# A layer's opening with four up blocks in turns over six PSUM banks, and one block's last rows inside the first seven-product block

## The chip, the cores and the metric

The kernel runs on one core of one Trainium2 chip. The metric is device time in microseconds, the median of several runs; a lower time is better. Of the engines, TensorE (PE, with PEld for its weight loads) multiplies, VectorE (DVE) and ScalarE (ACT) do the element-wise work, GpSimd (POOL) does small work and issues accumulating transfers, and SyncE (SP) issues the plain transfers in order.

## What is computed

One layer of a diffusion backbone on 256 latent tokens and 256 context tokens, width 2048, all in float32. The part that the change touches is the first half-step FFN with its modulation:

```python
mod_l = (silu_c @ w_mod[l] + b_mod[l]).reshape(B, N_MOD, D_MODEL)
mod_c = (silu_cc @ w_mod[l] + b_mod[l]).reshape(1, N_MOD, D_MODEL)
xl = half_step_ffn(xl, mod_l, 0, g_norm[l, 0], w_ffn1_up[l], w_ffn1_down[l])
xc = half_step_ffn(xc, mod_c, 0, g_norm[l, 0], w_ffn1_up[l], w_ffn1_down[l])

def half_step_ffn(x, mod, i, g, w_up, w_down):
    h = rms_norm(x, g) * (1 + mod[:, i + 1, None, :]) + mod[:, i, None, :]
    a, b = jnp.split(h @ w_up, 2, axis=-1)
    return x + 0.5 * mod[:, i + 2, None, :] * ((jax.nn.silu(a) * b) @ w_down)
```

Behind it come the token mixing (attention and mLSTM heads), a second FFN and a final RMSNorm, which the change leaves alone.

## The kernel before

**Products in three parts.** Every float32 operand is split into a rounded part hi and a rest lo (`split`: ACT makes hi, line 118, VectorE lo = raw - hi, line 119). A product of two split operands is three matmuls (`mm3`, lines 140 to 142): hi by hi, hi by lo, lo by hi. `split` draws from rings: three raw tiles of 1 MB, four hi and four lo tiles.

**The opening.** Context and latent tokens stand side by side as 512 columns. The 2048 rows of the width are 16 chunks of 128; `BLOCKS` takes them as (0,1), (1,2), (2,4), (4,6), ... (14,16). A block named by its first chunk k0 does this:

- *Modulation.* Shift SH and scale SC of its chunks come from `w_m0`, 32 units of 1 MB in the order of use (`mod_unit`, line 538, four buffers `mraw`). A pair block needs four units: one multiplied and summed on VectorE (the pair of 2.29 us operations), one for the other shift chunk and two for the scales, summed on PE with the conditions as stationary operand (`mod_sums`), copied by ACT to a row (line 558), transposed on PE and reduced on VectorE (`mod_turned`).
- *Hidden columns.* The normalised tokens `xs` are transposed on PE, and `affine_split` (lines 392 and 396) makes hhi (ACT) and hlo (VectorE) of them.
- *Up products.* `products` loads the block's rows of `w_up1` for both halves (a and b) of three hidden blocks f = 0, 1, 2 (line 425) and adds to six PSUM banks, one for each half of each f. A block's products run while the next block's modulation is made: six steps of six matmuls (three-matmul groups, pair by pair), put between the modulation sums.

In the opening VectorE, TensorE and the loads are pinned to program order (class `Pinned`, so their lines read L78); ACT is not. Before block 0 come the loads of the four token tiles, their sums of squares and scalings (`x_tile`), and `spread`, which broadcasts both conditions over the partitions: a diagonal on VectorE, four matmuls for each sequence, then copies to cB.

**Behind the opening.** `hidd` takes silu(a) * b of each f (`tail`, lines 666 to 668). The fourth block of the first group, f = 3, is loaded whole (line 133), split and multiplied in 96 matmuls. Then come nine groups of four hidden blocks by a seven-product scheme (`quad`); the first is called quad 1 here. It has 14 steps, each with a split and 24 matmuls; the operands a11, a12, a21, a22 are quarters of hhi and hlo, and n1, s2, s3, s4 are sums of them, made once by `token_forms` (lines 699 to 734) in 28 VectorE operations and some ACT copies: n1 ahead of quad 1, the others in its steps 1 to 6. n1 is used from step 4, s4 from step 6, s2 from step 8 and s3 from step 10. Its weights come in two `chain` tiles (`first_chain`, line 674), whose memory the opening's pool holds until its last operation, later added to by accumulating transfers from GpSimd (line 652). From here on a scheduler orders the instructions by readiness and program order.

## Time and profile before

| | us |
|---|---|
| median of 3 runs (lowest to highest) | 2656.78 (2656.41 to 2657.49) |
| profiled execution | 2654.22 |
| its span in the profile | 2652.5 |
| TensorE busy in the span | 2603.8 (98%) |
| VectorE busy | 2132.9 (80%) |
| ScalarE busy | 1349.5 (51%) |

The profile is of one execution. Busy time is the union of an engine's instructions; the profile models the ends of matmuls, which are pipelined. The views used are the page with its busy times, the table of windows (busy time, granted clock and DMA in chosen stretches), the groups of instructions with the idle time before them, the timeline and the waits of the transfer queue.

### The profile page before, as it was taken

To read this page: it belongs to the slowest core of one execution; us is meant where nothing else is said; L and a number is where in the kernel's file an instruction comes from. 1 tells how busy PE (TensorE), PEld (TensorE's weight loads), DVE (VectorE), ACT (ScalarE), POOL (GpSimd) and SP (SyncE) were. 2 spreads that over 40 slices of the span, in tenths; PEclk is the share of its full clock that TensorE was granted. 3 is DMA by queue.
4 is the path that set the end of the run, shared out by engine and by line. 5 is a ranking of instruction groups with operands and counts; after the bars stand their busy time and mean duration, and the time that the engine had idled before them with its cause. 6 is when DMAs were issued, how large, how long until landed. Compare 5 with 4: busy or idle time off the path is not lost. (4 is left out here: it accounts for less than half of the span.)

```text
span 2652.5 us, 33763 instructions
## 1 busy us (share of the span) xinstructions
PE 2603.8 (98%) x12718; PEld 2153.9 (81%) x12718; DVE 2132.9 (80%) x2918; ACT 1349.5 (51%) x1682; POOL 208.3 (8%) x259
## 2 busy tenths in 40 slices
PE   8999999999999999999999999999999999999998
PEld 4688887888888878888889888877898888888887
DVE  5697888878888788888886979797698777777877
ACT  4354444554444555444455336355476655555554
POOL 0000001000001100010110000111000000000001
PEclk9999999999999999999999999999999999999999
DMA  9979999999999988889986867574479998989975
GB/s 360 340 214 270 264 278 262 263 276 281 261 283 263 274 233 239 223 208 229 231 243 224 308 232 242 199 270 167 167 262 291 288 291 291 288 275 283 276 231 175
DMA packets 135028, 679.98 MB, mean 256 GB/s; under 512 B 14152, under 2 KB 23624, under 8 KB 73552
## 3 DMA queue, kind: packets, MB, share of 16 engines
q1 hardware_dynamic: 107216, 500.07, 50.8%
q0 software_dynamic: 27360, 177.22, 34.2%
q8 instruction: 100, 1.64, 0.2%
q10 hardware_dynamic: 288, 0.52, 0.1%
q14 instruction: 64, 0.52, 0.1%
HBM read 659.87 MB, written 17.89 MB: 256 GB/s over the span
## 5 line engine op out<-in xcount | busy, mean ns | idle before, releaser
L118 ACT ACTIVATE hi<-raw 128x1024 fp32r<-128x1024 f32 (+3 forms) x542 | 560.8, 1039 | 639.1 <-PE mm L142 481.8
L119 DVE TENSOR_TENSOR lo<-raw,hi 128x1024 fp32r<-128x1024 f32 (+1 forms) x524 | 631.1, 1211 | 272.2 <-ACT hi L118 254.9
L118 ACT ACTIVATE hi<-chain 128x1024 fp32r<-128x1024 f32 x320 | 337.9, 1059 | 257.6 <-PE mm L142 135.7
L119 DVE TENSOR_TENSOR lo<-chain,hi 128x1024 fp32r<-128x1024 f32 x320 | 387.5, 1221 | 95.8 <-ACT hi L118 93.1
L140 PE MATMUL mm<-hi,hhi 128*128 128x512 f32 (+3 forms) x1024 | 390.7, 384 | 7.3 <-DVE c L755 6.8
L141 PE MATMUL mm<-lo,hhi 128*128 128x512 f32 (+3 forms) x1024 | 387.6, 379 | 0.2
L142 PE MATMUL mm<-hi,hlo 128*128 128x512 f32 (+3 forms) x1024 | 387.0, 378 | 0.0
L211 DVE SCALAR_TENSOR_TENSOR junk<-sraw,cBh 128x1024 fp8e5<-128x1024 f32 x192 | 234.4, 1221 | 24.8 <-DMA sraw<-in_w_mt 22.5
L140 PEld LDWEIGHTS mm<-hi,hhi 128*128 128x128 f32 x1024 | 192.3, 188 | 40.0 <-ACT hi L118 6.4
L142 PEld LDWEIGHTS mm<-hi,hlo 128*128 128x128 f32 x1024 | 192.5, 188 | 33.6
L141 PEld LDWEIGHTS mm<-lo,hhi 128*128 128x128 f32 x1024 | 192.7, 188 | 32.0 <-DVE lo L119 1.3
L142 PE MATMUL mm<-hi,hid2l 128*128 128x512 f32 x352 | 137.4, 390 | 0.0
L140 PE MATMUL mm<-hi,hid2h 128*128 128x512 f32 x352 | 137.2, 390 | 0.0
L141 PE MATMUL mm<-lo,hid2h 128*128 128x512 f32 x352 | 137.1, 389 | 0.0
L140 PE MATMUL mm<-hi,h2hi 128*128 128x512 f32 x320 | 125.0, 391 | 1.5 <-DVE sab L1813 1.5
L141 PE MATMUL mm<-lo,h2hi 128*128 128x512 f32 x320 | 124.6, 389 | 0.0
L142 PE MATMUL mm<-hi,h2lo 128*128 128x512 f32 x320 | 124.6, 389 | 0.0
L652 POOL DMA_DIRECT2D chain<-in_w_up1b x60 | 53.1, 886 | 739.4 <-DVE lo L119 654.4
L142 PE MATMUL mm<-hhi,lo 128*128 128x512 f32 (+1 forms) x288 | 100.4, 349 | 4.5 <-DVE lo L119 4.4
L140 PE MATMUL mm<-hhi,hi 128*128 128x512 f32 (+1 forms) x288 | 101.3, 352 | 0.0
L141 PE MATMUL mm<-hlo,hi 128*128 128x512 f32 (+1 forms) x288 | 99.4, 345 | 0.0
L211 DVE SCALAR_TENSOR_TENSOR sr<-sr,cBl 128x1024 f32<-128x1024 f32 x72 | 87.1, 1216 | 7.0 <-DMA sr<-in_w_mt 6.8
(479 smaller groups left out, 5483.8 us busy)
## 6 DMA issues: line engine op xcount, KB each, us to landing
raw<-in_w_dn SPq DMA_DIRECT2D x70, 1024.0 KB, 7.3
sraw<-in_w_mt SPq DMA_DIRECT2D x128, 512.0 KB, 7.5
chain<-in_w_up1b POOLq DMA_DIRECT2D x60, 1024.0 KB, 11.1
raw<-in_w_up2b SPq DMA_DIRECT2D x50, 1024.0 KB, 7.0
raw<-in_w_up1b SPq DMA_DIRECT2D x40, 1024.0 KB, 8.5
sr<-in_w_mt SPq DMA_DIRECT2D x69, 512.0 KB, 5.3
mraw<-in_w_m SPq DMA_DIRECT2D x32, 1024.0 KB, 7.5
chain<-in_w_dn POOLq DMA_DIRECT2D x30, 1024.0 KB, 8.8
```

The costliest lines, as they stand in the source:

```text
L118: nc.scalar.activation(hi, src, AF.Copy)
L119: vector[0].tensor_tensor(lo, src, hi.bitcast(F32), op=ALU.subtract)
L140: tensor[0].matmul(out_ap, sh, mh, start=first, stop=False, skip_group_check=skip)
L141: tensor[0].matmul(out_ap, sh, ml, start=False, stop=False, skip_group_check=skip)
L142: tensor[0].matmul(out_ap, sl, mh, start=False, stop=last, skip_group_check=skip)
L211: ins = nc.vector.scalar_tensor_tensor(junk() if junk else raw, raw, 1.0, cB[s], op0=ALU.mult, op1=ALU.mult, accum_out=mT[:, i, s, kt, h : ...
L652: accum = lambda dst, src: nc.gpsimd.dma_start(dst, src, accum_op=ALU.add)
```

## The change

Four hidden blocks share the opening's six banks in turns. `COLUMN_PLAN` gives the blocks of f that each block of rows multiplies: 0, 1, 2 for rows up to chunk 4, then 1, 2, 3 up to chunk 10, then 2, 3, 0. When f = 0 has its chunks 0 to 3, and later f = 1 its chunks 0 to 9, the two banks are copied by ACT and written out to HBM by GpSimd (`PUT_BY`, `put_by`), and the banks go to f = 3 and to f = 0's second part. What a block missed is multiplied beside later blocks (`LATER`: f = 3's chunks 0 to 3 from block 6 on, f = 0's chunks 4 to 9 from block 12 on). The chunks 10 to 15 of f = 1 are multiplied within quad 1, in its steps 1 to 4, in two further PSUM banks. `whole_sums` copies a block's banks to SBUF and adds the part that was put by with an accumulating transfer; the tails of f = 0 and 1 then run at steps 4 and 7 of quad 1. The separate f = 3 goes.

`columns` takes the place of `products`: the same loads in one transfer where the f follow one another, else one for each f, and another order of matmuls: hi by hhi for all pairs of a load, then hi by hlo, then lo by hhi. The start of the opening is written out in `opening`: the first two modulation units are loaded ahead of block 0's weights, the latent condition is spread in four parts between other work, the sums of squares are shared by ACT and VectorE, and the scaling of each token tile beyond its first 256 columns is put off (`rest`) into the blocks 0 and 2.

```diff
 BLOCKS = ((0, 1), (1, 2)) + tuple((k, k + 2) for k in range(2, 16, 2))
+def _column_plan():
+    out = []
+    for k0, k1 in BLOCKS:
+        fs = (0, 1, 2) if k1 <= 4 else (1, 2, 3) if k1 <= 10 else (2, 3, 0)
+        out.append([[(f, k0, k1) for f in fs]])
+    return out
+COLUMN_PLAN = _column_plan()
+PUT_BY = {(0, 4): 3, (1, 10): 0}
+LATER = {6: [(3, 0, 4)], 12: [(0, 4, 8), (0, 8, 10)]}
 FB = 4
...
         return t if n == 2048 else t[:, :n]
-    def split(raw, n=2048):
-        half = n // 2
+    def split(raw, n=2048, count=2):
+        half = n // count
         parts = []
-        for h in range(2):
+        for h in range(count):
             hi = wp.tile([P, 1024], F32R, tag="hi", name="hi", bufs=4)[:, :half]
...
     pre = [[bank(), bank()] for _ in range(NPRE)]
+    slot = dict(enumerate(pre))
+    put_by = {f: [dr.tile([P, CB], F32, name=f"by{f}{ab}") for ab in range(2)] for f in (0, 1)}
     with pool(name="st", bufs=1) as st:
         scratch.append(st)
+        begun = set()
+        def columns(groups, early=False):
+            def load(g):
+                n = sum(2 * (k1 - k0) * P for _, k0, k1 in g)
+                raw = raw_tile(n)
+                o = 0
+                if len(g) > 1 and [f for f, _, _ in g] == list(range(g[0][0], g[0][0] + len(g))):
+                    f, k0, k1 = g[0]
+                    src = I["w_up1"][f : f + len(g), :, :, k0 * P : k1 * P].rearrange("f a p c -> p (f a) c")
+                    pin(nc.sync.dma_start(raw.rearrange("p (u c) -> p u c", u=2 * len(g)), src))
+                    return raw, n
+                for f, k0, k1 in g:
+                    w = 2 * (k1 - k0) * P
+                    pin(nc.sync.dma_start(raw[:, o : o + w].rearrange("p (a c) -> p a c", a=2), I["w_up1"][f, :, :, k0 * P : k1 * P].rearrange("a p c -> p a c")))
+                    o += w
+                return raw, n
+            ahead = load(groups[0])
+            if early:
+                wt = split(*ahead)
+            yield
+            for i, g in enumerate(groups):
+                if len(g) == 1:
+                    wt = split(*ahead, 1)
+                elif not early:
+                    wt = split(*ahead)
+                if i + 1 < len(groups):
+                    ahead = load(groups[i + 1])
+                each = [(f, ab, k) for f, k0, k1 in g for ab in range(2) for k in range(k0, k1)]
+                for f, _, _ in g:
+                    if f not in slot:
+                        slot[f] = [tbank(), tbank()]
+                done = 0
+                for wl, tl in ((0, 0), (0, 1), (1, 0)):
+                    for o, (f, ab, k) in enumerate(each):
+                        first = (f, ab) not in begun
+                        begun.add((f, ab))
+                        last = wl and (k == KT - 1 or (f, k + 1) in PUT_BY)
+                        tensor[0].matmul(slot[f][ab], wt(slice(o * P, o * P + P))[wl], (hhi, hlo)[tl][:, k, :], start=first, stop=bool(last))
+                        done += 1
+                        if done % (3 if g[0][2] - g[0][1] == 1 else 6) == 0:
+                            yield
+                for f, k0, k1 in g:
+                    if (f, k1) in PUT_BY:
+                        for ab in range(2):
+                            t = st.tile([P, 2, 256], F32, tag="h", name="by", bufs=2).rearrange("p a c -> p (a c)") if ab else st.tile([P, CB], F32, name="by", bufs=1)
+                            nc.scalar.activation(t, slot[f][ab], AF.Copy)
+                            nc.gpsimd.dma_start(put_by[f][ab], t)
+                            begun.discard((f, ab))
+                        del slot[f]
+                        slot[PUT_BY[f, k1]] = [bank(), bank()]
         cP = st.tile([P, KT, 32], F32, name="cP")
...
             return m
-        def spread(s, m):
-            for q in range(4):
-                b = pre[q // 2][q % 2]
-                w = slice(q * CB, (q + 1) * CB)
-                tensor[0].matmul(b, ones[:32, :], m[:, w], start=True, stop=True)
-                if s:
-                    nc.scalar.activation(cB[:, s, w], b, AF.Copy)
-                else:
-                    vector[0].tensor_copy(cB[:, s, w], b)
-        def x_tile(s, t, shared=False):
+        def spread(s, m, q, b):
+            w = slice(q * CB, (q + 1) * CB)
+            tensor[0].matmul(b, ones[:32, :], m[:, w], start=True, stop=True)
+            return lambda copy: copy(cB[:, s, w], b)
+        def x_sums(s, t, n_act):
             x = xs0[s, t]
...
             for cb in range(NCB):
-                if not (shared and cb % 2):
+                if cb < n_act:
                     sumsq(ss4[:, cb : cb + 1], x[:, cb * CB : (cb + 1) * CB])
...
             r = rsqrt_squares(ss4)
-            for c in (slice(0, 256), slice(256, D)):
-                vector[0].tensor_scalar(x[:, c], x[:, c], r, None, op0=ALU.mult)
+            return lambda c: vector[0].tensor_scalar(x[:, c], x[:, c], r, None, op0=ALU.mult)
         first_tb = pre[-1][-1]
...
                 tc.keep_in_program_order(nc.sync.dma_start(x, xsrc[s][t * P : (t + 1) * P, :]))
-        tc.keep_in_program_order(nc.sync.dma_start(vecs, I["vecs"]))
+        pin(nc.sync.dma_start(vecs, I["vecs"]))
         diagonals = [diagonal(s) for s in (CTX, LAT)]
-        spread(CTX, diagonals[0])
-        x_tile(CTX, 0)
-        x_turned(0, CTX, 0)
-        spread(LAT, diagonals[1])
-        for s, t in ((CTX, 1), (LAT, 0), (LAT, 1)):
-            x_tile(s, t, s == LAT and t == 1)
-            x_turned(0, s, t)
         def x_scaled(k, tb):
...
         unit = iter(range(32))
+        loaded = []
         def mod_unit():
+            if loaded:
+                return loaded.pop(0)
             raw = st.tile([P, 2048], F32, tag="mraw", name="mraw", bufs=4)
...
             turns.clear()
-        turns = []
-        for k0, k1 in BLOCKS:
+        turns, back, rest = [], iter(()), []
+        loaded.extend([mod_unit() for _ in range(2)])
+        def opening(following):
+            banks4 = [pre[q // 2][q % 2] for q in range(4)]
+            wide = [spread(CTX, diagonals[0], q, banks4[q]) for q in range(4)]
+            late = lambda q: spread(LAT, diagonals[1], q, (pre[2][0], banks4[0])[q] if q < 2 else tbank())(lambda o, x: nc.scalar.activation(o, x, AF.Copy))
+            for n, (s, t) in enumerate(xs0):
+                scaled = x_sums(s, t, 2 if n else 3)
+                wide[n](vector[0].tensor_copy)
+                scaled(slice(0, 256))
+                rest.append(lambda scaled=scaled: scaled(slice(256, D)))
+                if n == 3:
+                    drain(mod_sums(0, 0, 1))
+                x_turned(0, s, t)
+                for q in {1: (0,), 2: (1,)}.get(n, ()):
+                    late(q)
+            mod_turned()
+            drain(mod_sums(1, 0, 1))
+            steps(following)
+            mod_turned()
+            for q in (2, 3):
+                late(q)
+        for (k0, k1), groups in zip(BLOCKS, COLUMN_PLAN):
             kk = slice(k0, k1)
-            following = products(I["w_up1"], pre, k0, k1, hhi, hlo, k0 == 0)
+            following = columns(groups, k0 == 0)
+            if k0 in LATER:
+                back = columns([[x] for x in LATER[k0]])
+                steps(back)
             if k1 - k0 == 2:
                 raw = mod_unit()
-            for i in range(2):
+            if not k0:
+                opening(following)
+            for i in range(2 if k0 else 0):
                 for _ in mod_sums(i, k0 if i else k1 - 1, k1, following if i else iter(())):
                     steps(prods, 3 - (k1 - k0))
-                if k0 == 0:
-                    mod_turned()
+                    steps(back)
+                    if k0 == 2 and rest:
+                        rest.pop(0)()
                 if not i and k1 - k0 == 2:
...
             mod_turned()
+            while k0 == 2 and rest:
+                rest.pop(0)()
             steps(prods)
...
                 x_scaled(k0, tb)
+                if not k0:
+                    rest.pop(0)()
+                    rest.pop(0)()
             else:
...
         drain(prods)
+        drain(back)
         vector[0], tensor[0] = nc.vector, nc.tensor
...
             return f1u.tile([P, CB], F32, tag="ca", name="ca", bufs=2)
-        def tail(f, pab):
-            sa = ca_tile()
-            nc.scalar.activation(sa, pab[0], AF.Silu)
-            nc.vector.tensor_tensor(sa, sa, pab[1], op=ALU.mult)
+        def tail(f, a, b, sa):
+            nc.scalar.activation(sa, a, AF.Silu)
+            nc.vector.tensor_tensor(sa, sa, b, op=ALU.mult)
             nc.sync.dma_start(hidd[0][:, :, f, :], sa.rearrange("p (t c) -> p t c", t=4))
+        def whole_sums(f):
+            out = [c12_tile() if f else f1u.tile([P, CB], F32, tag="cy", name="cy", bufs=2) for _ in range(2)]
+            for x, b, before in zip(out, slot[f], put_by[f]):
+                nc.scalar.activation(x, b, AF.Copy)
+                accum(x, before)
+            return out
         def part(n, ab, c):
...
             first_chain(1, c)
-        for f in range(NPRE):
-            tail(f, pre[f])
-        for f in range(NPRE, FB):
-            pab = []
-            for ab in range(2):
-                wt = load_split(I["w_up1"][f, ab])
-                b = bank()
-                for k in range(KT):
-                    mm3(b, *wt(slice(k * P, (k + 1) * P)), hhi[:, k, :], hlo[:, k, :], k == 0, k == KT - 1)
-                pab.append(b)
-            tail(f, pab)
+        def c12_tile():
+            return f1u.tile([P, CB], F32, tag="c12", name="c12", bufs=2)
+        for f in (2, 3):
+            tail(f, *slot[f], ca_tile())
+        first_of = {0: whole_sums(0)}
         n1, s2, s4 = form("n", "n1"), form("s", "s2"), form("t", "s4")
...
         mul = lambda o, x, y: nc.vector.tensor_tensor(o, x, y, op=ALU.mult)
-        def c12_tile():
-            return f1u.tile([P, CB], F32, tag="c12", name="c12", bufs=2)
         def quad(n, after=lambda step: None):
...
         def first_steps(step):
+            if step == 0:
+                steps(back)
+            if step in (1, 2, 3):
+                steps(back, 2)
+            if step == 4:
+                drain(back)
+                tail(0, *first_of[0], first_of[0][0])
+                first_of[1] = whole_sums(1)
+            if step == 7:
+                tail(1, *first_of[1], first_of[1][0])
             if step in (1, 2, 3, 4, 5, 6):
...
         raws, place0 = [], []
+        back = columns([[(1, 10, 14)], [(1, 14, 16)]])
         quad(1, first_steps)
...
```

## The prediction

> **What bounds the kernel now.** I read the page first, for the engine that fills the span.
>
> ```profile
> span 2652.5 us, 33763 instructions
> PE 2603.8 (98%) x12718; PEld 2153.9 (81%) x12718; DVE 2132.9 (80%) x2918; ACT 1349.5 (51%) x1682; POOL 208.3 (8%) x259
> ```
>
> TensorE is busy for 98% of the span. A change that keeps its matmuls can only win the time in which it stands still. So the next view is the table of windows, cut at the starts of the opening's blocks and at the first seven-product block ("quad 1"). Its columns: window, its length, then for PE, PEld, DVE, ACT, POOL the busy time with a count, then clock, DMA share and GB/s.
>
> ```profile
> 0.00:29.60 29.60, 20.48 (x119) 9.10 (x119) 16.48 (x32) 17.00 (x43) 4.01 (x21) 1.00 0.92 358
> 29.60:46.50 16.90, 15.35 (x136) 9.58 (x136) 9.01 (x19) 4.82 (x11) 0.00 (x0) 0.90 0.90 339
> 46.50:61.00 14.50, 12.44 (x106) 8.17 (x106) 10.28 (x22) 5.09 (x10) 0.00 (x0) 1.00 0.97 370
> 61.00:74.70 13.70, 13.45 (x112) 9.21 (x111) 9.70 (x17) 5.09 (x10) 0.00 (x0) 1.00 1.00 370
> 102.00:116.80 14.80, 13.45 (x112) 9.21 (x111) 9.70 (x17) 5.09 (x10) 0.00 (x0) 1.00 0.98 354
> 130.50:144.10 13.60, 12.40 (x58) 9.83 (x57) 11.25 (x14) 6.10 (x11) 0.00 (x0) 1.00 0.55 209
> 144.10:166.00 21.90, 21.90 (x98) 18.16 (x97) 21.90 (x20) 10.39 (x12) 1.04 (x1) 1.00 0.82 242
> 166.00:242.00 76.00, 76.00 (x340) 62.95 (x340) 61.62 (x68) 37.62 (x42) 7.08 (x8) 1.00 0.86 232
> ```
>
> Three things stand here. In the opening PE is idle, most of it early. At the same time the DMA share is 0.90 to 1.00, so a block of 13.7 us is nearly full on both sides. And from 144.1 us PE has no idle time at all: block f=3 (144.1 to 166.0) and quad 1 run without a gap, but beside f=3 VectorE is busy for 21.90 of 21.90 us. Which waits make up the opening's idle time is in the groups of PE instructions from 0 to 144 us; the last part of a row is the idle time before the group.
>
> ```profile
> L78 PE MATMUL mm<-hhi,hi 128*128 128x512 f32 x96 | 41.9, 436 | 1.1 <-ACT hhi L392 1.1
> L78 PE MATMUL mm<-hhi,lo 128*128 128x512 f32 x96 | 38.8, 404 | 2.0 <-DVE lo L78 2.0
> L78 PE MATMUL mm<-hlo,hi 128*128 128x512 f32 x96 | 38.3, 399 | 3.0 <-DVE hlo L78 3.0
> L78 PE MATMUL tr<-mraw,cP 128*32 128x256 f32 x224 | 15.0, 385 | 1.9 <-DMA mraw<-in_w_m 1.9
> L78 PE MATMUL mm<-raw,ones 32*128 32x512 f32 x16 | 14.4, 1076 | 2.5 <-DVE raw L78 2.5
> L78 PE MATMUL tr<-mraw,cP 128*32 128x128 f32 x352 | 13.6, 302 | 0.3 <-DVE h L78 0.3
> L78 PE MATMUL tr<-ident,row 128*128 128x128 f32 x25 | 4.5, 277 | 0.8 <-ACT row L558 0.8
> L78 PE MATMUL mm<-ident,xs 128*128 128x128 f32 x4 | 1.4, 456 | 1.9 <-DVE xs L78 1.9
> L465 PE MATMUL tr<-ident,cc 32*128 32x32 f32 x1 | 0.3, 279 | 2.8 <-ACT cc L194 2.8
> ```
>
> Idle in all: 1.1+2.0+3.0+1.9+2.5+0.3+0.8+1.9+2.8 = **16.3 us**. The last row and the wait for the diagonals (2.5) come before anything the change touches, so 11.0 can be won. Busy spans are modelled past the next start, so gaps are somewhat longer than shown:
>
> ```profile
> 144.08 0.39 PE L140 MATMUL mm<-hhi,hi 128*128 128x512 f32 x1
> 144.30 0.39 PE L141 MATMUL mm<-hlo,hi 128*128 128x512 f32 x1
> 135.37 0.49 PE L78 MATMUL mm<-hlo,hi 128*128 128x512 f32 x1 [0.83 <-DVE hlo L78]
> 136.24 0.50 PE L78 MATMUL mm<-hhi,lo 128*128 128x512 f32 x1 [0.37 <-DVE lo L78]
> ```
>
> Streaming matmuls start 0.22 to 0.23 us apart, while one with a gap behind it is charged 0.49: each gap hides up to 0.27 us more, some 4 us over about 15 gaps.
>
> **The change part by part.**
>
> *The matmul count is conserved.* Before: 288 products in the opening (three groups of 96) and 96 for f=3. After, by the plan: f=0, 2, 3 get all 16 rows in the opening and f=1 ten, 58 rows of 6 matmuls = 348, and quad 1 takes the 6 missing rows, 36. At 0.227 us the opening grows by 60 x 0.227 = 13.6 us, quad 1 by 8.2, and the 21.8 us of f=3 go: zero. Spreads, modulation sums and transposes keep their number too. The whole effect is idle time won and lost.
>
> *Product order (hi by hhi for all pairs, then hlo, then lo): gain.* The waits for hlo and lo are 3.0+2.0 us. In a pair block 12 matmuls now stand ahead of the first that needs hlo (2.7 us) and 24 ahead of the first that needs lo (5.4 us); the longest wait, 0.83 us, is covered. With 0.27 us for nine such gaps this is 5.0+2.4 = 7.4 us at most. I take 5.5, since the early ones partly turn into waits for transfers (below).
>
> *Front: gain.* The first product starts at 29.60, where the first window ends; only after that does PE run steadily. In the new order PE no longer takes all eight spreads (14.4 us) before the first modulation sum; two go behind it, under the chain row, SC, hhi. I put the first product near 23.5 us. But 4 wide scalings and the second block's work meet on VectorE in block 2:
>
> ```profile
> L78 DVE TENSOR_SCALAR xs<-xs,rstd 128x1792 f32<-128x1792 f32 x4 | 4.6, 1148 | 0.0
> L78 DVE SCALAR_TENSOR_TENSOR junkv<-mraw,cB 128x2048 fp8e5<-128x2048 f32 x14 | 32.0, 2288 | 0.2
> 46.45 1.09 PE L78 MATMUL tr<-ident,xs 128*128 128x128 f32 x8
> ```
>
> Two scalings (2.3 us) stand in line with block 2's pair of 2.29 us sums ahead of its transposes (46.45 now). So of a lead of some 6 us about 4.2 is left there; I take **4.2**, bounds 2 and 6.
>
> *Transfers: loss.* The change adds to the opening 10 rows of reads (1.31 MB) and four partial sums out (1.05 MB): 2.36 MB at 370 GB/s = 6.4 us of a DMA that is 0.90 to 1.00 busy. All loads stand in SP's one ordered queue, so an added load delays the mraw units behind it.
>
> ```profile
> 56.81 1.07 PE L78 MATMUL tr<-mraw,cP 128*32 128x256 f32 x16 [0.77 <-DMA mraw<-in_w_m]
> 112.65 1.07 PE L78 MATMUL tr<-mraw,cP 128*32 128x256 f32 x16 [1.12 <-DMA mraw<-in_w_m]
> 126.29 1.07 PE L78 MATMUL tr<-mraw,cP 128*32 128x256 f32 x16
> 137.60 0.60 ACT L666 ACTIVATE ca<-mm 128x512 f32<-128x512 f32 x1 [2.41 <-PE mm L78]
> ```
>
> The front's lead pulls PE ahead of transfers that hardly can come sooner, so waits of about 1 us come in blocks 4 and 6 (where a 0.52 MB load and the first partial sums join). From block 8 on the 24 and then 36 extra matmuls (5.5 and 8.2 us) give the DMA more time than its extras take, and the 1.12 us wait goes. Sum **-0.7**, bounds 0 and -6. The opening's balance: 5.5+4.2-0.7 = **9.0 us won**, bounds 4 and 12. The added ACT copies (8 of about 0.6 us, half of them behind the opening) lie in ACT's idle time, which is over half of each block; uncovered they would cost 5.
>
> *The hand-over to quad 1: loss.* Today f=3's 21.9 us hide three things: the chains' landing, the tails, and the token forms on VectorE. That cover goes.
>
> ```profile
> 135.52 0.80 SPq L674 DMA_DIRECT2D chain<-in_w_up1b  x2
> 149.49 1.07 ACT L118 ACTIVATE hi<-chain 128x1024 fp32r<-128x1024 f32 x1 [0.28 <-PE mm L141]
> SPq L674 <- DVE hlo L78: 11.5, 1, 11.5
> DMA to landing us min/median/max: 4.8/7.2/8.2
> L119 DVE TENSOR_TENSOR lo<-chain,hi 128x1024 fp32r<-128x1024 f32 x8 | 9.7, 1220 | 0.5 <-ACT hi L118 0.5
> L699 DVE TENSOR_TENSOR sraw<-sraw,hlo 128x1024 f32<-128x1024 f32 x8 | 9.7, 1218 | 0.0
> L667 DVE TENSOR_TENSOR ca<-ca,mm 128x512 f32<-128x512 f32 x4 | 2.7, 680 | 0.0
> 151.51 1.22 DVE L119 TENSOR_TENSOR lo<-chain,hi 128x1024 fp32r<-128x1024 f32 x1
> 152.65 1.22 DVE L700 SCALAR_TENSOR_TENSOR sraw<-sraw,hhi 128x1024 f32<-128x1024 f32 x1
> ```
>
> Let H be the end of the last hlo. The chain load is issued 0.2 us after H, because it waits for hlo, and lands 4.8 us later at best: H+5.0. PE ends the last products about 7 us after H (36 x 0.227 = 8.2, begun 1.2 earlier). The first half's hi takes 1.07 (ACT) and lo 1.22 (VectorE): H+7.3 if VectorE is free, so nearly no wait. But from H it has 1.8 us of the block's own lo, then the first form n1, 8 operations at a pitch of 1.14 (151.51 to 152.65) = 9.1 us, and two tails, 1.2 us. All of these stand ahead of the first chain's lo in the program. If all go first, lo ends at H+13.3 and PE waits 6.3 us; if none, 0.5. The two halves of n1 wait for ACT between, so some lo slips in; nearest to the order seen in the trace, where VectorE runs forms as fast as they come, I take **4.5**.
>
> *Quad 1: small loss.* The two late loads bring 1.2 and 0.7 us of VectorE splits, four accumulating transfers go on POOL's queue (8% busy), and the four sums borrow the buffers of cy and c12, on which ACT's in-order copies may wait for a store. VectorE's work up to the eighth step (forms 28 x 1.14 = 32, splits 9 x 2.3 = 20, tails, adds) ends near H+57, PE gets there near H+59 (8 x 24 x 0.227 + 8.2 = 52 from H+7): close, but in time. I take **0.7**, bounds 0 and 3.
>
> Sum: -9.0+4.5+0.7 = **-3.8 us**. The profiled execution took 2654.22, 1.7 more than its span and 2.56 below the median 2656.78; the difference is put on the median: **2653.0**.
>
> One rule is weighed against this. The clock was cut once in the opening:
>
> ```profile
> 29.60:36.00 6.40, 5.59 (x43) 3.79 (x44) 1.22 (x2) 1.22 (x4) 0.00 (x0) 0.73 0.96 376
> ```
>
> It was granted 0.73 over these 6.4 us, after the idle stretches of the front, a loss of 1.7 us; no such cut follows at 144 us. A wait of 4 us or more at the hand-over could bring another 1.7; I leave it out of the sum and put it into the slower case. The Trainium skill ("TensorE: Matmul & The Clock Gate", "What's actually happening") says that an idle window of about 3.4 us halves the clock; by that rule the sum would be -2.1 instead of -3.8.
>
> **The rivals.**
> 1. *A clean hand-over.* VectorE takes the chain's lo as soon as it lands: wait 1.5, quad 1 at 0.3. -9.0+1.8 = -7.2: **2649.6**. For it: before, chain lo (151.51) ran in the middle of the forms. Against: program order.
> 2. *The opening is bound by transfers.* PE's lead is taken back by the mraw units behind 6.4 us of added traffic; the opening wins 4, the hand-over takes 4.5, quad 1 0.7: +1.2, **2658.0**. For it: shares of 0.97 to 1.00. Against: from the last unit's sums (126.29) PE still has some 18 us of work until 144.08.
> 3. *Slower: VectorE bounds quad 1.* The forms stay ahead of the splits: 6.3 at the hand-over and 1.7 of clock. VectorE then enters steps 3 to 6 without a lead, where it has 14 form operations (16.0), four splits (9.2) and some five adds and tails (3.0), 28.2 us, against PE's 4 x 24 x 0.227 = 21.8: 6.4 more. With 7.5 won in the opening: +6.9, **2663.7**. It decides where these losses pass the opening's gain by 5.3. For it: 21.90 of 21.90 us. Against: only n1 is due by step 4, and each step's split stands ahead of that step's form.
>
> **How the numbers follow.** Forecast 0.45, clean hand-over 0.30, transfers 0.15, slower 0.10. 0.2% is 5.3 us, about what a measurement of this kernel can tell from no change. Faster by more: the clean case and a fifth of the forecast's (0.39); slower by more: the last (0.10); the rest 0.51. The range goes from a won 10.5 (12 less 1.5) to a loss of 3: 2646.3 to 2660.0.
>
> **What would show it.** In the profile after: 348 and 36 products; hardly a row "<-DVE hlo" or "<-DVE lo" on PE before the hand-over; block 2's transposes near 42 us; the opening's products ending near 149 (144.1+13.6-9); then a PE gap before the first X matmul, put down to lo of the chain, of 3 to 6 us. The forecast is wrong if PE waits for mraw for more than 4 us in the opening, if that gap is under 2 us, or if PE waits again and again for lo within quad 1.

## The result and the profile after

The changed kernel took **2675.36 us** (median of 4 runs, 2670.83 to 2677.55), the kernel before 2656.6 beside it; the ratio is **1.0068** with a 95% interval of 1.0056 to 1.008. It is slower by 18.8 us; the forecast of 2653.0 and its range to 2660.0 are missed. The profiled execution took 2674.02 us; a trace is of one execution, and those of one kernel differ by some microseconds.

The profile's page of the changed kernel: TensorE has the same 12718 matmuls, and the span is 19.8 us longer.

```profile
span 2672.3 us, 33819 instructions
PE 2613.6 (98%) x12718; PEld 2160.8 (81%) x12718; DVE 2136.0 (80%) x2929; ACT 1349.0 (50%) x1681; POOL 213.1 (8%) x267
```

The table of windows, cut again at the blocks' starts and behind the opening (columns as in the prediction):

```profile
0.00:28.80 28.80, 23.06 (x119) 9.99 (x119) 16.00 (x39) 13.76 (x32) 4.00 (x21) 1.00 0.93 368
46.00:63.50 17.50, 13.54 (x105) 9.08 (x106) 10.28 (x22) 6.15 (x11) 0.00 (x0) 0.90 0.96 369
108.50:132.60 24.10, 19.41 (x130) 13.78 (x129) 10.83 (x18) 6.81 (x13) 1.07 (x2) 0.86 0.88 332
132.60:149.90 17.30, 17.30 (x130) 12.66 (x129) 10.30 (x18) 5.09 (x10) 0.00 (x0) 1.00 0.12 49
162.00:193.00 31.00, 26.06 (x104) 20.02 (x103) 27.75 (x27) 16.77 (x20) 3.57 (x4) 0.94 0.99 281
193.00:250.00 57.00, 51.40 (x213) 41.70 (x214) 44.03 (x49) 25.73 (x30) 7.01 (x8) 0.94 0.91 225
```

Before, PE was busy without a gap and at full clock from 144.1 to 242 us. Now it lacks 4.9 us in the 31 after the opening and 5.6 in the next 57, at a clock of 0.94. In the opening the stretch in which block 12's modulation is made (108.5 to 132.6) has a hole and a clock of 0.86, and right behind it the transfers stand nearly still (0.12). The groups of PE instructions from 0 to 162 us:

```profile
L91 PE MATMUL mm<-hlo,hi 128*128 128x512 f32 x116 | 33.4, 427 | 0.0
L91 PE MATMUL tr<-mraw,cP 128*32 128x128 f32 (+1 forms) x576 | 31.1, 356 | 9.8 <-DMA mraw<-in_w_m 9.4 <-DVE h L91 0.3
L91 PE MATMUL mm<-hhi,lo 128*128 128x512 f32 x116 | 29.8, 398 | 0.0
```

The new product order took away every wait of the opening for hlo and lo (3.0 and 2.0 us before), and the wait for modulation units grew from 1.9 to 9.4. The timeline of PE's larger waits, with the idle time and its releaser in brackets:

```profile
45.97 1.10 PE L91 MATMUL tr<-ident,xs 128*128 128x128 f32 x8 [2.16 <-DVE SH L91]
57.75 1.87 PE L91 MATMUL tr<-mraw,cP 128*32 128x256 f32 x16 [3.63 <-DMA mraw<-in_w_m]
124.91 1.94 PE L91 MATMUL tr<-mraw,cP 128*32 128x256 f32 x16 [4.70 <-DMA mraw<-in_w_m]
161.73 0.77 PE L153 MATMUL mm<-hi,hhi 128*128 128x512 f32 x2
166.78 0.54 PE L154 MATMUL mm<-lo,hhi 128*128 128x512 f32 x1 [4.28 <-DVE lo L132]
194.21 1.93 PE L517 MATMUL tr<-hhi,lo 128*128 128x512 f32 x4 [1.85 <-DVE lo L132]
234.65 0.50 PE L153 MATMUL mm<-hi,s2h 128*128 128x512 f32 x1 [3.63 <-ACT hi L131]
```

The opening's products end, and quad 1 begins, at 161.7 us. With no gain and no loss they would end at 144.1 + 13.6 = 157.7. So in this execution the opening lost 4.0 us where 9.0 were to be won. The hand-over costs 4.28, as forecast, and quad 1 waits twice more. Two rows among these take 1.87 and 1.94 us where the same group took 1.07 before: that is the half clock which follows a wait. A window around the largest shows it:

```profile
122.70:129.50 6.80, 4.59 (x22) 2.75 (x23) 0.00 (x0) 0.38 (x1) 0.00 (x0) 0.50 1.00 418
```

The clock was 0.50 for 6.8 us. Such cuts stand at the waits of 57.8, 124.9, 166.8, 194.2 and 234.7 us. By the four windows above with a clock under 1 they take 17.5 x 0.10 + 24.1 x 0.14 + 31 x 0.06 + 57 x 0.06 = 10.4 us of full clock, a part of it while PE waited anyway.

Where the wait of 4.70 comes from stands in the timeline of the transfer queue from 105 to 118 us:

```profile
106.44 0.33 SPq L596 DMA_DIRECT2D mraw<-in_w_m  x1
106.82 0.66 SPq L703 DMA_DIRECT2D ccd<-cc  x1
115.10 1.41 SPq L492 DMA_DIRECT2D raw<-in_w_up  x3
117.00 1.30 SPq L596 DMA_DIRECT2D mraw<-in_w_m  x3
```

and in the waits of that queue (total, times, longest):

```profile
SPq L492 <- DVE lo L91: 7.5, 1, 7.5
```

SP's queue stood 7.5 us on a load of up rows (line 492), which waited for VectorE's lo to free a raw tile: block 12's rows and its two `LATER` loads want more than the ring's three tiles. Behind it stood the modulation unit that PE wanted, issued at 117.0.

### The profile page after: what moved, and what is told of

Read it like the earlier page. It is cut to its first block, busy times and chain, and to the rows that moved or that the text cites. A ratio compares the mean times of both kernels' runs of the same rounds, so it can differ in the third digit from the quotient of the medians.

```text
span 2672.3 us, 33819 instructions
## 1 busy us (share of the span) xinstructions
PE 2613.6 (98%) x12718; PEld 2160.8 (81%) x12718; DVE 2136.0 (80%) x2929; ACT 1349.0 (50%) x1681; POOL 213.1 (8%) x267
## 5 line engine op out<-in xcount | busy, mean ns | idle before, releaser
L131 ACT ACTIVATE hi<-raw 128x1024 fp32r<-128x1024 f32 (+4 forms) x543 | 561.4, 1037 | 644.2 <-PE mm L155 486.2
L132 DVE TENSOR_TENSOR lo<-raw,hi 128x1024 fp32r<-128x1024 f32 (+3 forms) x522 | 628.1, 1210 | 271.2 <-ACT hi L131 254.4
L746 POOL DMA_DIRECT2D chain<-in_w_up1b x60 | 52.9, 882 | 592.2 <-DVE lo L132 477.1
L155 PE MATMUL mm<-hhi,lo 128*128 128x512 f32 (+1 forms) x256 | 88.0, 344 | 4.5 <-DVE lo L132 4.4
L153 PE MATMUL mm<-hhi,hi 128*128 128x512 f32 (+1 forms) x256 | 88.7, 347 | 0.0
L154 PE MATMUL mm<-hlo,hi 128*128 128x512 f32 (+1 forms) x256 | 86.8, 339 | 0.0
```

Of the source, the lines that this page charges most:

```text
L131: nc.scalar.activation(hi, src, AF.Copy)
L132: vector[0].tensor_tensor(lo, src, hi.bitcast(F32), op=ALU.subtract)
L153: tensor[0].matmul(out_ap, sh, mh, start=first, stop=False, skip_group_check=skip)
L154: tensor[0].matmul(out_ap, sh, ml, start=False, stop=False, skip_group_check=skip)
L155: tensor[0].matmul(out_ap, sl, mh, start=False, stop=last, skip_group_check=skip)
L746: accum = lambda dst, src: nc.gpsimd.dma_start(dst, src, accum_op=ALU.add)
```

## The experiments

All times are medians with their number of runs; a ratio is to the kernel before on the same chip, with its 95% interval. The medians of the kernel before, taken beside the runs, lie between 2655.1 and 2656.9, so ratios are compared.

**1. The blocked queue.** f = 0's late rows come in one load, one raw tile instead of two.

```diff
-LATER = {6: [(3, 0, 4)], 12: [(0, 4, 8), (0, 8, 10)]}
+LATER = {6: [(3, 0, 4)], 12: [(0, 4, 10)]}
...
-                    wt = split(*ahead, 1)
+                    wt = split(*ahead, 1 if ahead[1] <= 1024 else 2)
```

> Only f = 0's six late rows come in one load and one raw tile in place of two; bytes and matmuls are the same. Theory A (three raw tiles: in the changed kernel the load of block 12's rows waited from 106.8 to 115.1 us for a raw tile, and the mraw units stood behind it in SP's queue): the PE wait of 4.70 us at 124.91 goes down to under 1.5, the cut of the clock near 122.7 (6.8 us at half, 3.4 us of work) goes with it, and the time falls by 5 to 8 us, to about 2667 to 2670. Theory B (the DMA has too much to carry with the added 2.36 MB): the wait stays above 3.5 us and the time within 2 us of the changed kernel's.

Measured: 2667.32 (10 runs), ratio 1.0039 [1.0026, 1.0053], against 1.0068 [1.0056, 1.008]. The wait at 124.9 and its cut are gone; the same place in the table of windows:

```profile
103.00:120.00 17.00, 17.00 (x130) 12.42 (x129) 11.16 (x19) 6.67 (x14) 1.07 (x2) 1.00 0.99 372
```

PE is busy for all of it at full clock. The medians differ by 8.0 us. From block 10's transposes (108.5 us in the changed kernel) to quad 1's first product 53.2 us pass there, 53.1 and 52.9 in the traces of runs 5 and 3, which have the same opening, and 46.4 here. So the blocked queue cost some 7 us in the traces: 4.7 by the wait, and the rest nearly all by the clock, as run 2 shows.

**2. What the clock costs.** The changed kernel with 20 matmuls of no use (4.7 us) ahead of the modulation sum that waited 4.70; their bank is read by nothing.

```diff
                 raw = mod_unit()
+                if g and k1 == 14:
+                    d = tbank()
+                    for j in range(20):
+                        tensor[0].matmul(d, hhi[:, j % 8, :P], hhi[:, j % 8, :], start=True, stop=True)
```

> The changed kernel with 20 more matmuls of 512 columns (4.5 us at the streaming pace), on data that is there, into a PSUM bank that nobody reads, just ahead of the last modulation sum of block 12, where PE waits 4.70 us for mraw at 124.91. Theory A (the clock is cut because PE stands still for some 4 us): PE is busy in the wait, the sum begins at the same time within 0.5 us, the cut of 6.8 us near 122.7 does not come, and the kernel with more work is 2 to 4 us faster than the changed one. Rival (the cuts come from something else and only fall near the waits): the cut stays, and the time is the same or up to 1 us longer.

Measured: 2670.06 (4 runs), ratio 1.0057 [1.0035, 1.0079]; the interval overlaps the changed kernel's, so the 5 us between the medians is not settled by the ratios alone. The trace shows the mechanism: the unit's sum follows at once and takes 1.07 us instead of 1.94.

```profile
115.94 4.70 PE L91 MATMUL tr<-hhi 128*128 128x512 f32 x20
120.60 1.07 PE L91 MATMUL tr<-mraw,cP 128*32 128x256 f32 x16
```

The wait is filled and the cut behind it is gone. The stretch named in run 1 takes 50.9 us instead of 53.2, so 2.3 us are won though PE does more; the rest of the difference between the medians is not shown to come from this edit.

**3. The forms behind the chain's lo.** The first two steps of `token_forms` move from ahead of quad 1 into its step 0.

```diff
-        steps(forms, 2)
         turn = []
...
-            if step in (1, 2, 3, 4, 5, 6):
+            if step in (0, 1, 2, 3, 4, 5, 6):
                 steps(forms)
```

> Only the place of the token forms changes: n1 is made in steps 0 and 1 of quad 1 and each later form one or two steps later, behind the split of the step. Theory A (at the hand-over the chain's lo stands behind n1's operations on VectorE): the PE wait of 4.28 us at 166.78 falls to 0.5 to 2, the cut of the clock near 167.1 (1.7 us) goes, and the time falls by 4 to 6 us, about 2668 to 2670, if the later forms still come in time. Rival (the chain's landing sets the start): the wait stays at 3 us or more. A third way: forms come late in steps 4 to 8, with PE waits for n1, s4 or s2, and the gain is given back.

Measured: 2675.85 (4 runs), 1.0071 [1.0049, 1.0093]: nothing won. The wait for the chain's lo fell from 4.28 to under 0.2, but now PE came 11.10 us too early for something else:

```profile
178.24 2.07 PE L517 MATMUL tr<-hhi,hi 128*128 128x512 f32 x4 [11.10 <-ACT hi L131]
```

That was ScalarE's hi, late by a load:

```profile
177.13 1.06 ACT L131 ACTIVATE hi<-raw 128x1024 fp32r<-128x1024 f32 x1 [11.63 <-DMA raw<-in_w_up]
```

and the loads of line 492 there landed after

```profile
DMA to landing us min/median/max: 16.3/17.1/18.0
```

f = 1's late rows, loads of 0.5 and 0.25 MB, took 16.3 to 18.0 us from issue to landing. So behind the wait for the chain's lo stands the next one, for these rows.

**4. The old front**, in the changed kernel: spreads, sums and scalings ahead of block 0 as before.

```diff
...
-            if not k0:
-                opening(following)
-            for i in range(2 if k0 else 0):
+            for i in range(2):
...
```

> The start of the opening as before (eight spreads ahead of the first modulation sum, full scalings, no units loaded ahead), all else as changed. Theory A (the new front wins nothing: the clock stays at half until 30.6 us in place of 25.0, and the deferred scalings hold block 2's sums on VectorE, so that one wait for mraw of 3.63 us with a cut of 1.7 stands at 57.75): the time is the same within 2 us or up to 4 us less, and block 4's transposes stand at 60 to 62 us in place of 63.55. Rival (the new front wins its 4 us as forecast, the loss is elsewhere): 3 to 5 us more, 2677 to 2679.

Measured: 2673.48 (4 runs), 1.0064 [1.0041, 1.0087]. The front is worth nothing that can be measured here.

**5. Own tile for the second tail's result**, so that ScalarE's copies need not wait for its store.

```diff
+            o = chp.tile([P, CB], F32, tag="stg", name="stg") if f == 1 else sa
-            nc.vector.tensor_tensor(sa, sa, b, op=ALU.mult)
+            nc.vector.tensor_tensor(o, sa, b, op=ALU.mult)
...
```

> Only the result of f = 1's tail goes to another SBUF tile, from which it is stored; the two c12 tiles come free when VectorE has read them. Theory A (ACT stood 9.1 us at the copy to c12, whose tile the store held until 232.97): that ACT wait goes, the PE waits of 3.63 and 0.76 us at 234.65 go, and the cut of the clock near 235.4 (1.7 us) too: 5 to 6 us less than the changed kernel, about 2669. Theory B (VectorE's backlog of forms is what makes hi and lo late there): a PE wait of 3 us or more for lo or hi stays between 228 and 240 us and the time stays within 2 us.

Measured: 2670.95 (6 runs), 1.006 [1.0041, 1.0079]. ScalarE no longer waited for the store, but PE waited 5.96 us at the same place, by its timeline:

```profile
235.28 0.77 PE L153 MATMUL mm<-hi,hhi 128*128 128x512 f32 x1 [5.96 <-DVE c L851]
```

and VectorE's:

```profile
233.30 1.23 DVE L224 SCALAR_TENSOR_TENSOR junk<-sraw,cBh 128x1024 fp8e5<-128x1024 f32 x1 [7.06 <-DMA sraw<-in_w_mt]
234.45 0.68 DVE L851 TENSOR_TENSOR c<-mm,c 128x512 f32<-128x512 f32 x1
```

VectorE stood 7.06 us on the tile `sraw` of the modulation that runs beside the quads, with the add that frees the bank behind it. `sraw` is loaded by SP's queue right behind that store. The intervals of this kernel and the changed one overlap, so no gain is measured.

**6. All the small cures at once** (runs 1, 3 and 5, two spreads later, and the put-off scalings on ScalarE):

```diff
-            for q in (2, 3):
-                late(q)
...
                 if not k0:
+                    late(2)
+                    late(3)
...
-            return lambda c: vector[0].tensor_scalar(x[:, c], x[:, c], r, None, op0=ALU.mult)
+            return lambda c: nc.scalar.activation(x[:, c], x[:, c], AF.Copy, scale=r) if c.start else vector[0].tensor_scalar(x[:, c], x[:, c], r, None, op0=ALU.mult)
```

> The changed kernel with all of these: one load for f = 0's late rows, the store of f = 1's tail from a tile of its own, the forms later, the third and fourth part of the latent spread behind the first block's columns, and the deferred scalings on ACT in place of VectorE. Theory A (the four waits with their cuts and the front make up the loss): no PE wait over 2 us behind 62 us, no cut of the clock between 62 and 260 us, 15 to 22 us less than the changed kernel: 2653 to 2660, about level with the kernel before or some us faster. Rival (the waits move on to the next late thing): 6 to 12 us less, with a new PE wait of over 2 us named in the profile.

Measured: 2670.0 (4 runs), 1.0055 [1.0037, 1.0072]. The rival held in the trace: PE waited 10.17 us at 171.8 for the late rows and 3.98 near 227. The time is 5.4 us below the changed kernel, a little less than the rival's 6 to 12, and no better than run 1 alone. Next, the same with the old front and without the last two edits:

> As the kernel with four things mended, but with the start of the opening as before. Theory A: within 3 us of that one; if the new front with its two mends wins, up to 4 us more than it, and if the old front with full clock from 25 us is the better start, up to 3 us less.

Measured: 2669.52 (4 runs), 1.0053 [1.0032, 1.0074], the same time.

**7. The product order alone**, put into the kernel before.

```diff
-                for k in range(k0, k1):
...
-                    mm3(b, *wt(w), hhi[:, k, :], hlo[:, k, :], k == 0, k == KT - 1)
...
+            for wl, tl in ((0, 0), (0, 1), (1, 0)):
+                for u in range(nu):
...
+                    for k in range(k0, k1):
...
+                        tensor[0].matmul(b, wt(w)[wl], (hhi, hlo)[tl][:, k, :], ...)
```

> The kernel before with one edit: the order of a block's product matmuls (hi by hhi for all six pairs, then by hlo, then lo by hhi). Theory A (the waits for hlo and lo, 3.0 and 2.0 us, go, but from block 4 on the transfers pace the opening, so that only the wait at the end, 1.6 us from start to start at 135, and part of the others are won): 1 to 4 us less than before, 2653 to 2656. Rival (all of the idle time there is won): 5 to 7 us less. Third: PE's lead turns into waits for mraw of over 3 us with a cut of the clock: no gain or a loss of up to 2.

Measured: 2650.82 (10 runs), 0.999 [0.9977, 1.0004]. The profiled execution took 2658.84, 8 us above the median, so its waits need not stand in the others. In it the waits for hlo and lo are gone, but PE runs into a unit:

```profile
113.58 1.93 PE L78 MATMUL tr<-mraw,cP 128*32 128x256 f32 x16 [2.97 <-DMA mraw<-in_w_m]
```

with a half clock behind it (1.93 for a group of 1.07). The queue's timeline:

```profile
99.42 0.33 SPq L542 DMA_DIRECT2D mraw<-in_w_m  x1
99.80 0.43 SPq L425 DMA_DIRECT2D raw<-in_w_up  x1
100.32 0.49 SPq L542 DMA_DIRECT2D mraw<-in_w_m  x1
```

That unit (100.32) stands in SP's queue behind 1.5 MB of up rows (99.80) that are wanted only in the next block.

**8. Up rows behind the last unit**, with the product order, in the kernel before.

```diff
+                raw = mod_unit()
                 if g == KT // nk - 1:
                     steps(last)
-                raw = mod_unit()
```

> The kernel before with the new order of the products, and each block's load of up rows issued behind the block's last modulation unit instead of ahead of it. Theory (the wait of 3.1 us near 113 us and its cut come from the 1.5 MB of up rows that stand ahead of a unit which is wanted sooner): that wait is under 1 us, no cut near 113 us, and the time is 4 to 6 us below the kernel before, a ratio of 0.998 or less. Rival (the transfers as a whole are late at that place, so that the next unit waits instead): a wait of 2 to 3 us stays within a unit or two, and the ratio is about 0.999, as with the new order alone.

Measured: **2647.43** (7 runs), **0.9967 [0.9955, 0.9979]**, the fastest kernel here and faster than both. The window from 30 us to the end of the opening's products:

```profile
30.00:137.00 107.00, 103.77 (x857) 74.23 (x858) 78.45 (x138) 43.19 (x84) 0.00 (x0) 1.00 0.94 359
```

and the span of the profiled execution (2642.21 us, 5 us below the median) with its mean clock (0.994 in the changed kernel):

```profile
core 0: 2640.5 us, clock 0.999
```

From 30 to 250 us no wait of PE is longer than 1.52 us, and between the first 27 and the last 8 us the clock is never cut. The new order of loads without the new order of products was not tried.

**9. Rows ahead of quad 1** (with run 1's one load). f = 1's late rows are loaded at the end of the opening, where the transfers stood still, and multiplied right behind its products; both partial sums come back ahead of quad 1 and the tails run at steps 1 and 2.

```diff
+                last_rows = columns([[(1, 10, 14)], [(1, 14, 16)]])
+                steps(last_rows)
...
+        drain(last_rows)
...
-        first_of = {0: whole_sums(0)}
+        first_of = {0: whole_sums(0), 1: whole_sums(1)}
```

> The kernel with the one load, and beside it the second block's missing rows taken out of quad 1: their loads are issued at the end of the opening, their 36 matmuls follow the opening's products, and both partial sums are returned and both tails run at quad 1's first steps. Theory (the place of the rows is the cost: the chain's lo is late because nothing stands between the opening and quad 1, and quad 1's splits wait for rows, stores and sums that come in its midst): the wait of 4.4 us before quad 1 is gone, covered by 8.2 us of products, the waits of 1.1 and 2.0 us near 180 us and the 5.5 us near 225 us shrink below 2 us together, and the time is 2652 to 2658 us. Rival (the accumulating transfers keep the queues busy whatever the order): the wait of some 5 us near 225 us, with a cut of 6.8 to 10.2 us, stays, only the hand-over is won, and the time is 2661 to 2665 us.

Measured: 2664.29 (10 runs), 1.0021 [1.0006, 1.0035]. The time is in the rival's range, but the trace fits neither: the hand-over's wait is gone, that near 225 us fell to 2.08 us without a cut, and 3.6 us of waits stand at 177 and 180 us.

**10. The store in a queue of its own** (with runs 1 and 5): the tails of f = 0 and 1 are stored by ScalarE's queue.

```diff
-            nc.sync.dma_start(hidd[0][:, :, f, :], ...)
+            (nc.sync, nc.scalar)[f < 2].dma_start(hidd[0][:, :, f, :], ...)
```

> The kernel with the one load and the result of the second block's tail in a tile of its own, and the stores of the tails of f = 0 and 1 issued by ScalarE instead of SyncE. Theory (the store of f = 1's tail, 512 short rows that take turns with the accumulating transfers for some 25 us, holds the sraw loads that stand behind it in the same queue; VectorE waits for sraw in order, and quad 1's lo stands behind it): the second sraw lands within 12 us of its issue as the first did, the wait of 5.5 us near 225 us and its cut are gone, and the time is 2659 to 2663 us. Rival (sraw is slow because the accumulating transfers take the DMA engines, whichever queue): sraw still takes about 20 us, the wait stays, and the time is 2666 to 2670 us.

Measured: 2661.63 (10 runs), 1.0015 [1.0002, 1.0029]; the theory held. In run 1 the wait of 5.36 us near 225 us begins on ScalarE, whose copy waits for the store to free its tile, which run 5's edit cures:

```profile
223.22 0.60 ACT L872 ACTIVATE c<-mm 128x512 f32<-128x512 f32 x1 [10.82 <-DMA hid<-c]
```

With that cured, run 5 showed the wait for `sraw`, which the store's own queue is to cure. From issue to landing, the `sraw` loads of 190 to 226 us in run 1 (shortest, median, longest), then the store there:

```profile
DMA to landing us min/median/max: 11.1/13.5/19.9
```
```profile
DMA to landing us min/median/max: 25.8/25.8/25.8
```

and the same two in this run:

```profile
DMA to landing us min/median/max: 10.1/10.8/11.4
```
```profile
DMA to landing us min/median/max: 28.0/28.0/28.0
```

The store of 0.25 MB is as slow in its own queue, but nothing waits behind it: `sraw` lands in 11.4 us at worst, and the wait near 225 us and its cut are gone. The 5.7 us below run 1 are for the tile and the queue together. The Trainium skill ("DMA: Bandwidth & Descriptors", "Queues, rings and completion order") says that a DMA engine takes turns between the queues it has work for, a packet from each; the trace agrees, in that the other queue's loads no longer wait for this store.

**11. Rows ahead and the store's queue together** (runs 9, 5 and 10):

> The kernel with the second block's rows ahead of quad 1, and beside it the store of the first two tails issued by ScalarE and the second tail's result in a tile of its own. Theory (late chain lo and the short-row store are two separate causes): both gains of the two runs before add up, 3 and 5.7 us below the kernel with the one load, and the time is 2655 to 2660 us, level with the kernel before. Rival (with the rows ahead of quad 1 the tails store before the heaviest accumulating traffic, so the second cause is gone already): no wait is left for this to remove, the waits of 4 us near 177 us stay, since they come from a plain load beside four accumulating transfers, and the time is 2662 to 2666 us.

Measured: 2661.5 (8 runs), 1.0027 [1.0016, 1.0037], between the two ranges. The trace is the rival's: the two gains do not add, and waits of 4.21 and 2.15 us stand near 180 us, behind a load of quad 1 that took 17 us.

**12. The order of loads in the mended kernel**: run 8's edit in run 11's kernel.

> The kernel with the rows ahead of quad 1 and the stores on ScalarE's queue, and each block's load of up rows issued behind the block's last modulation unit, as in the run on the kernel before. Theory (the opening of the changed kernel, too, waits for units that stand behind up rows in the queue): the waits of 2.5 and 3.3 us near 37 and 51 us fall below 2 us together, the opening's products end 3 to 4 us sooner, and the time is 2656 to 2659 us. Rival (there the transfers as a whole are late, and what is won before 60 us is lost in quad 1, whose loads set the pace): the time stays at 2660 to 2663 us.

Measured: 2663.26 (10 runs), 1.0018 [1.0006, 1.0029]. The rival held: the waits only moved (3.30 at 46, 2.33 at 64.5, 4.62 and 1.91 near 183 us).

**13. Plain return of the partial sums**, all else as in 12: a plain transfer, and VectorE adds the bank.

```diff
-                nc.scalar.activation(x, b, AF.Copy)
-                accum(x, before)
+                nc.gpsimd.dma_start(x, before)
+                nc.vector.tensor_tensor(x, x, b, op=ALU.add)
```

> As e13, and the put-by partial sums come back by plain transfers of GpSimd's queue into the tile, to which VectorE adds the bank, instead of accumulating transfers onto a copy of the bank. Theory (the accumulating transfers of 1 MB in all delay the plain loads of quad 1's first splits, which take 17 us): the load that landed after 17.1 us lands within 12 us, the waits of 4.4 and 2.5 us near 177 us fall below 3 us together with at most one short cut, and the time is 4 to 6 us below e13's. Rival (it is the chain's own accumulating transfers, which the kernel before has too): that load still takes 15 us or more and the time is within 2 us of e13's.

Measured: **2655.16** (10 runs), 1.0 [0.999, 1.0009]: 8.1 us below run 12. The two loads of quad 1 issued from 150 to 165 us (the middle figure is the mean of two) landed after

```profile
DMA to landing us min/median/max: 8.2/12.7/17.2
```

in run 12 and after

```profile
DMA to landing us min/median/max: 8.7/10.2/11.8
```

here, and the waits near 180 us are gone but for 1.65.

**14. The old front once more**, in this kernel (run 4's edit):

> The kernel with the plain return of the partial sums and all that went with it, and the start of the opening as in the kernel before: both conditions spread and the four token tiles scaled whole ahead of block 0's products. Theory (the new front's put-off work only moves VectorE's work under blocks 2 and 4, where it makes the products wait): the waits of 3.5 and 2.2 us at 42 and 62 us fall below 2 us together, the cut near 65 us is gone, and the time is 2650 to 2654 us. Rival (the front is worth the 4.2 us forecast for it and the waits stand in front of work that is late anyway): the time is 2657 to 2661 us. Between the two the front is worth nothing either way.

Measured: 2657.26 (10 runs), 0.9999 [0.9986, 1.0012]. The waits at 42 and 62 us (3.31 and 2.07 in run 13) fell to 0.63 and 1.65 and the cut went, but the time is the same as with the new front; a wait of 4.09 at 247.9, with a cut, came up instead. The front is worth nothing that can be measured either way.

## Why the prediction was wrong

- **"The matmul count is conserved": right.** 348 and 36 products, the same 12718 matmuls.
- **"Product order: gain 5.5": mechanism right, but no gain that is clear by itself.** All waits for hlo and lo went (run 7 too), and run 7 is 0.999 [0.9977, 1.0004]. In its profiled execution, 8 us above its median, what was won came back as a wait for the next unit, 2.97 us with a cut; whether the others have that wait is not shown. With the loads reordered too (run 8) the time is 0.9967 of before, some 8 us less: more than the term and near the 7.4 given as the most, but the opening's cut (1.7 us by the prediction's sum) went as well. The intervals of runs 7 and 8 just touch.
- **"Front: gain 4.2": failed.** The first product starts at 28.8 instead of 29.6, not near 23.5, and runs 4 and 14 measure nothing. PE did come earlier to its work, the first modulation sum at 17.8 us (before: 23.0), but it worked at half clock until 30.6 us (before: 25.0): the last sum ahead of the first product, before and after, is

```profile
27.37 1.08 PE L78 MATMUL tr<-mraw,cP 128*32 128x128 f32 x32
```
```profile
26.96 1.94 PE L91 MATMUL tr<-mraw,cP 128*32 128x128 f32 x32
```

  (The table of windows has a clock of 1.00 there, since the trace's records of the clock begin only with the change to full.) When the clock first comes full is in part luck: in the traces it is 21.7 to 32.2 us with the new front and 25.0 to 34.9 with the old. But the clock is not the whole failure. In run 10 the clock came full at 22.6 us and the first product starts at 26.74; in run 14, with the old front, it came at 25.1 and the product starts at 29.66. Block 2's transposes (the `xs` rows) in run 10, with the largest wait ahead of them, and in run 14:

```profile
39.99 1.94 PE L91 MATMUL tr<-mraw,cP 128*32 128x256 f32 x16 [2.40 <-DMA mraw<-in_w_m]
44.23 1.03 PE L91 MATMUL tr<-ident,xs 128*128 128x128 f32 x8
```
```profile
43.89 1.09 PE L91 MATMUL tr<-ident,xs 128*128 128x128 f32 x8 [0.63 <-DVE SH L91]
```

  So even then the lead was 2.9 us, not six, and block 2 has none of it: in run 10 PE waits 0.47 and 2.40 us for modulation units ahead of it, the second time with a cut. Such waits were named under the transfers, but of about 1 us and only for blocks 4 and 6.
- **"Transfers: loss 0.7": failed, with the largest wait.** It counted bytes against the bandwidth. It named the one ordered queue, but not that a load in it can wait for a raw tile: 7.5 us, price 7 to 8 us with the clock (run 1). Bytes were not the limit there: run 1 moves the same bytes without that wait, and right behind block 12's stretch the DMA share is 0.12. The wait of 3.63 us at 57.8 is not settled: the share is 0.96 around it, and the same wait is 2.0 and 0.9 us in runs 3 and 5. With 9.4 us of waits for units in all, the prediction's own sign of being wrong (more than 4) came. The opening's balance of 9.0 won became 4.0 lost in this trace; the same opening in runs 3 and 5 ends at 158.3 and 155.5 instead of 161.7, and without the blocked queue (run 1) at 150.4, which is 7.3 won. So most of the miss of 22.4 us lies in this queue and behind the opening.
- **"Hand-over: 4.5": right in size (4.28) and cause** (n1's forms stand ahead of the chain's lo), but the wait was not the last in line: without it, PE waits for the next load instead (runs 3 and 6).
- **"Quad 1: 0.7": failed.** The step weighed VectorE's work against PE's and gave the accumulating transfers no time, since POOL is 8% busy; it named ScalarE's copies that may wait for a store, but priced all of it at 0.7. How busy POOL is does not show what they cost: beside them plain transfers are late. The loads of `sraw` from 180 to 226 us, before and after:

```profile
DMA to landing us min/median/max: 3.0/7.2/10.3
```
```profile
DMA to landing us min/median/max: 11.1/11.7/18.6
```

  The waits in quad 1 come to some 6 us, with cuts; the store's tile and queue (run 10) and the accumulating return (run 13) were worth 5.7 and 8.1 us. Run 10 and run 1, and 12 and 13, have intervals that just overlap, so these two sizes are rough; the traces show both causes, and from run 1 to run 13, whose intervals lie apart, the medians fall by 12.2 us.
- **The clock left out of the sum: failed.** The Trainium skill's rule ("TensorE: Matmul & The Clock Gate", "What's actually happening") that was weighed and set aside said that the hand-over's wait would bring a cut. It did (half clock from 167.1 us), and so did four other waits.
- **The rivals.** None reached the measured time. "Bound by transfers" (2658.0) was nearest in the opening, but for the queue and not, where it was tested, for the bandwidth. "VectorE bounds quad 1" had the right sign and the wrong engine: in quad 1 VectorE waited for transfers (run 5).

What stays open: runs 13 and 14 stand at the level of the kernel before, run 8 some 8 us below it, though all three have the new product order and the new order of loads. Their traces differ in some waits of 2 to 4 us between 180 and 250 us; which part of the four blocks in turns makes these was not told apart.

## What to carry to other kernels

A transfer is not costed by its bytes alone: ask what it waits for, since in an ordered queue that holds everything behind it, and issue what is wanted soonest first. Removing block work that "hides" other things removes the time in which the next stage's loads, sums and splits get ready, and curing the first wait shows the next. A new order that saves waits on one resource may show its gain only when the next resource, here the modulation units, is moved up as well.

## What the runs showed of the hardware

**Whether a wait cuts the clock depends on where it falls.** All changes of the granted clock in the trace of the changed kernel, after it first became full at 30.56 us, lie at whole multiples of 3.41 us from there (the cut of 6.8 us above is two such steps, from 122.72, 27 steps on). In run 12 a wait of 3.30 us was not followed by a cut, and one of 2.33 was:

```profile
46.14 1.10 PE L91 MATMUL tr<-ident,xs 128*128 128x128 f32 x8 [3.30 <-DVE SH L91]
64.51 1.66 PE L91 MATMUL tr<-mraw,cP 128*32 128x128 f32 x32 [2.33 <-DMA mraw<-in_w_m]
```

The two windows around them have a clock of 1.00 and 0.66:

```profile
41.00:50.00 9.00, 5.36 (x56) 3.89 (x56) 7.16 (x15) 4.70 (x9) 0.00 (x0) 1.00 0.92 364
64.00:69.00 5.00, 4.49 (x40) 3.62 (x41) 4.97 (x6) 0.69 (x2) 1.32 (x2) 0.66 1.03 406
```

So a wait below 3.4 us can cost a cut and one of nearly that length need not. The steps tell them apart. Counted from run 12's first full clock at 30.73 us, steps end at 44.38, 61.45 and 64.86 us. The wait of 3.30 us (42.84 to 46.14) falls over two steps, with at most 1.76 us of it in one; that of 2.33 (62.18 to 64.51) lies whole in one, and the half clock begins where that step ends. In all the traces here each cut from full clock follows a step in which PE was idle for 1.97 us or more, by its busy time; steps with up to 2.51 us idle passed without one. The Trainium skill ("TensorE: Matmul & The Clock Gate", "What's actually happening") has a free-running window of 3.4 us, and a half clock behind an idle one. The steps agree with the window; the one ahead of run 12's cut was not idle throughout.

**A small store beside accumulating transfers took 25 to 28 us** for 0.25 MB (24.7 in run 5, 25.8 in run 1, 28.0 in run 10). Its rows are 512 bytes long; that this makes it slow was not tried.
